# Seven products instead of eight in the gate and up projections of a two-layer decoder trunk

## The chip, the cores and the metric

The kernel runs on one core of one Trainium2 chip. The time is device time in microseconds for one execution, the median of repeated runs. Names of engines in the profile: PE is the matrix engine (TensorE) and PEld its weight loads, DVE is VectorE, ACT is ScalarE, POOL is GpSimd, SP is SyncE, on whose queue all transfers are issued.

## The reference

The program is a decoder trunk of 2 layers on 512 tokens of width 1024. Each layer is: x + 0.5·FFN1, a mixing part (a convolution group, a gated short convolution, a sparse attention group that keeps the 128 best keys), cross-attention into 256 memory tokens, x + 0.5·FFN2. A final RMS norm ends it. The part that the change touches is the FFN, four times in all (two per layer), with hidden width 2816:

```
def swiglu(h, w_gate, w_up, w_down):
    return (jax.nn.silu(h @ w_gate) * (h @ w_up)) @ w_down

x = x + 0.5 * swiglu(rms_norm(x, ffn1_norm[l]), ffn1_w_gate[l], ffn1_w_up[l], ffn1_w_down[l])
```

## The kernel before

Everything is kept transposed: features lie on the 128 partitions and the 512 tokens along the row. The 1024 features of x are 8 tiles X[0] to X[7], the 2816 hidden features are 22 columns of 128.

**Three matmuls for one product.** Every float32 factor is split into a high part that the matrix engine takes as it is (ACT copies it, rounded) and a low part (DVE subtracts the high part from the value). `mm3` then issues three matmuls: high·high, high·low, low·high. Each has its own weight load. A column of gate or up over 8 feature tiles is so 8·3 = 24 matmuls of 128x512.

**The norm.** `Norm.chunk` splits each x tile times its gain into `norm.h`; the factor 1/rms of each token (`norm.rb`) comes late, from `finish`: a sum of squares by POOL and PE, a power on POOL, and two matmuls with `ones_r` that spread it over the partitions. `norm.rb` is multiplied onto the gate and, after the down projection, onto the result.

**The FFN.** `ffn` works in two parts of 12 and 10 hidden columns (`HALVES`). In a part it first walks over column pairs: four weight blocks of 128x1024 (gate and up, two columns each) are loaded into `stg`, split into `whi` and `wlo`, and two columns of gate and two of up are computed. `gated` multiplies the gate by `norm.rb`, takes its silu, multiplies by up and splits the result into `hid`. Then the down projection of the part adds into X, in column pairs `mp`; the last part also calls `nxt.chunk`, which prepares the next norm. The first FFN of layer 0 begins with `begin`, which computes the first pair while x and the weights still arrive.

**What sets the order.** All operations are recorded first, as the functions call them. `Plan.order` then sorts them for all engines together: it gives each operation a cost and a due time (from the place of the matmuls that need it) and starts, engine by engine, the operation that is ready earliest, among equals that with the earliest due time. Buffers are counted: `stg` has 4, `whi` and `wlo` 3 each (NW), `s` 70 (NSLOT, 128x512 each), `ps` the 8 banks of PSUM. Each engine then executes its list strictly in this order, waiting on semaphores. Nearly all instructions show the same line (345 before, 353 after), the line that issues the sorted list; they are told apart by tiles and shapes.

Of the kernel before, what the change touches and what calls it, by code (L numbers as in the profile page):

```python
# [55 lines left out]
def _columns(c0, c1, k0=0, nk=DC, first=()):  # L56
    r, c = [], c0
    while c < c1:
        n = min(first[0] if first else P, c1 - c)
        first = first[1:]  # L60
        r.append((k0, nk, c, n))
        c += n
    return r


def _rows(c0, c1):
    return [(k, 2, c, T) for c in range(c0, c1, T) for k in range(0, DC, 2)]

BLOCKS = {"w_in": _columns(0, O_V) + _rows(O_V, O_QI) + _columns(O_QI, O_KI) + _columns(O_KI, N_IN, first=(68,)),
          "w_out": _columns(0, D), "xa_wq": _columns(0, D), "xa_wo": _columns(0, D),
          "xa_wkv": _columns(0, D) + _rows(D, 2 * D)}
for _name in ("ffn1", "ffn2"):
    BLOCKS[_name + "_w_gate"] = BLOCKS[_name + "_w_up"] = _columns(0, F, first=(2 * P,))
    BLOCKS[_name + "_w_down"] = [b for f0, nf in HALVES for i in range(2)
                                 for b in _columns(0, D, f0 + i * nf // 2, nf // 2)]

TWO_PI = 2.0 * math.pi  # L80
C1 = 6.28125
# [267 lines left out]
def trunk_kernel(ctx: ExitStack, tc: tile.TileContext, a: dict, out: bass.AP):  # L349
# [16 lines left out]
    def planned(pool, tag, w, dt):  # L366
        return nc.tile(tag, (P, w), dt, lambda: pool.tile([P, w], dt, tag=tag, name=nm(tag), bufs=nc.tags[tag]["bufs"]))
# [28 lines left out]

    def mm3(o, w, x, start, stop):
        nc.tensor.matmul(o, w[0], x[0], start=start, stop=False)
        nc.tensor.matmul(o, w[0], x[1], start=False, stop=False)
        nc.tensor.matmul(o, w[1], x[0], start=False, stop=stop)  # L400
# [36 lines left out]
    def pcol(name, i):  # L437
        return cols[:, COLS[name] + i:COLS[name] + i + 1]
# [65 lines left out]
    def block(w, k0, nk, c0, n):  # L504
        name, l = w
        at = 0
        for b0, bk, bc, bn in BLOCKS[name]:
            if b0 <= k0 and k0 + nk <= b0 + bk and bc <= c0 and c0 + n <= bc + bn:
                b = a[name][l][:, at:at + bk * bn].rearrange("p (k c) -> p k c", k=bk)
                return b[:, k0 - b0:k0 - b0 + nk, c0 - bc:c0 - bc + n]  # L510
            at += bk * bn

    def load(w, k0, nk, c0, n):

        stg = planned(wpool, "stg", 1024, F32)[:, :nk * n].fold(nk)
# [9 lines left out]
    def part(w, k, n=P):  # L525
        return w[0][:, k, :n], w[1][:, k, :n]


    def ffn(l, which, norm, nxt, begin=None, end=None):
        wg, wu, wd = ((f"{which}_w_{n}", l) for n in ("gate", "up", "down"))  # L530
        for f0, nf in HALVES:
            hid = []

            def gated(pg, pu):
                g = slot()
                nc.vector.tensor_mul(g, pg, norm.rb)
                s = slot()
                nc.scalar.activation(s, g, AF.Silu)
                nc.vector.tensor_mul(g, pu, s)
                hid.append(split(g))  # L540

            if begin and f0 == 0:
                begin(wg, wu)
                norm.finish()
                for ob in opening:
                    gated(*ob)
            for b in range(1 if begin and f0 == 0 else 0, nf // 2):
                c0 = (f0 + 2 * b) * P
                wgt = load_cols(wg, c0)
                wut = load_cols(wu, c0)  # L550
                for i in range(2):
                    pg, pu = bank(), bank()
                    for wt, o in ((wgt[i], pg), (wut[i], pu)):
                        for k in range(DC):
                            mm3(o, part(wt, k), norm.h[k], k == 0, k == DC - 1)
                    if f0 == 0 and b == 0 and i == 0:
                        norm.finish()
                    gated(pg, pu)
            for mp in range(DC // 2):
                kh = nf // 2  # L560
                ws = [load_cols(wd, mp * 256, 256, f0 + i * kh, kh) for i in range(2)]
                halves = end and f0 and mp == DC // 2 - 1
                for x in (slice(0, T // 2), slice(T // 2, T)) if halves else (slice(0, T),):
                    for i in range(2):
                        m = 2 * mp + i
                        o = bank()[:, x]
                        for k in range(nf):
                            mm3(o, part(ws[k // kh][i], k % kh), tuple(t[:, x] for t in hid[k]), k == 0, k == nf - 1)
# [567 lines left out]
```

## Time and profile before

| | us |
|---|---|
| median of 3 runs | 2278.47 (2278.05 to 2279.54) |
| the profiled execution | 2280.02 |
| its span, first to last instruction | 2278.2 |
| PE busy in the span | 2246.0 |
| DVE busy | 1273.3 |
| ACT busy | 844.8 |
| mean granted TensorE clock | 0.991 of full speed |

The program holds 10354 matmuls and as many weight loads. A busy time is the union of an engine's records. A matmul's record is longer than the step from one matmul to the next, since they are pipelined: the pace is read from start to start. DVE records also overlap a little with the next one.

### The profile page before, as it was taken

The page shows a single profiled execution, that of the slowest core. Times are in us where ns is not written, and L with a number is a line of the kernel's source. Part 1 is how long each engine was busy: PE and PEld are TensorE (multiplying, and loading weights), DVE is VectorE, ACT ScalarE, POOL GpSimd, SP SyncE. Part 2 cuts the span into 40 slices and gives each one's busy share as a digit, 9 for nine tenths or more (in the row PEclk, how much of TensorE's full clock was granted, in tenths as well). Part 3 has the DMA queues.
Part 4 walks back from the last instruction along what each step waited for, and adds up shares of the span by engine and source line. Part 5 has one row for each costly group of instructions (what it writes and reads, how often), then busy time and mean ns, then how long its engine had stood idle before and what let it go on. Part 6 is the DMA issues. An engine that isn't in the chain of part 4 may idle for free. (4 is left out here: it accounts for less than half of the span.)

```text
span 2278.2 us, 26623 instructions
## 1 busy us (share of the span) xinstructions
PE 2246.0 (99%) x10354; PEld 1854.7 (81%) x10354; DVE 1273.3 (56%) x2026; ACT 844.8 (37%) x1308; POOL 149.9 (7%) x111
## 2 busy tenths in 40 slices
PE   8999999998999999999999999999999999999998
PEld 7888888787688888888888888878787888888887
DVE  7334347999855544343543334469998554343434
ACT  5222334326834433222332223333377343222322
POOL 2000001101020200000100000020100101000001
PEclk9999999999999999999999999999999999999999
DMA  6333323445332232332333343243543313323322
GB/s 219 96 84 109 100 78 99 121 118 151 92 95 64 84 101 81 102 104 85 101 102 97 83 115 90 81 132 97 139 124 99 93 56 93 102 81 113 93 76 82
DMA packets 88335, 229.70 MB, mean 101 GB/s; under 512 B 10128, under 2 KB 23568, under 8 KB 88208
## 3 DMA queue, kind: packets, MB, share of 16 engines
q1 hardware_dynamic: 88208, 228.00, 34.8%
q8 instruction: 81, 1.33, 0.2%
q14 instruction: 46, 0.38, 0.1%
HBM read 211.70 MB, written 2.10 MB: 94 GB/s over the span
## 5 line engine op out<-in xcount | busy, mean ns | idle before, releaser
L345 PE MATMUL ps<-s,whi 128*128 128x512 f32 (+1 forms) x5896 | 1767.9, 385 | 0.0
L345 PEld LDWEIGHTS ps<-s,whi 128*128 128x128 f32 x5896 | 1098.2, 188 | 224.6 <-issue 4.4
L345 PE MATMUL ps<-s,wlo 128*128 128x512 f32 (+1 forms) x2948 | 1106.2, 384 | 0.0
L345 ACT ACTIVATE whi<-stg 128x1024 fp32r<-128x1024 f32 (+2 forms) x430 | 420.6, 979 | 1221.8 <-PE ps L345 1017.1
L345 PEld LDWEIGHTS ps<-s,wlo 128*128 128x128 f32 x2948 | 553.6, 188 | 108.9
L345 DVE TENSOR_TENSOR wlo<-stg,whi 128x1024 fp32r<-128x1024 f32 (+2 forms) x430 | 484.6, 1128 | 133.3 <-ACT whi L345 133.2
L345 DVE TENSOR_TENSOR s<-ps,s 128x512 f32<-128x512 f32 (+1 forms) x264 | 181.3, 690 | 566.1 <-PE ps L345 542.5
L345 POOL TENSOR_TENSOR s<-s,s 128x512 f32<-128x512 f32 (+1 forms) x88 | 134.7, 1534 | 1916.8 <-ACT s L345 1657.8
L345 ACT ACTIVATE s<-s 128x512 fp32r<-128x512 f32 (+2 forms) x255 | 157.0, 626 | 92.3 <-DMA s<-s 45.1
L345 PE MATMUL ps<-s,s 128*128 128x512 f32 (+7 forms) x688 | 162.0, 375 | 16.5 <-DVE s L345 12.1
L345 DVE TENSOR_TENSOR s<-s,s 128x512 fp32r<-128x512 f32 (+3 forms) x206 | 149.0, 732 | 7.7 <-ACT s L345 6.7
L345 DVE SCALAR_TENSOR_TENSOR s<-ps,s 128x512 f32<-128x512 f32 (+1 forms) x70 | 47.2, 676 | 187.4 <-PE ps L345 187.4
L345 PEld LDWEIGHTS ps<-s,s 128*128 128x128 f32 (+1 forms) x688 | 111.0, 187 | 46.4 <-DVE s L345 15.2
L345 ACT ACTIVATE s<-ps 128x512 fp32r<-128x512 f32 (+4 forms) x192 | 93.5, 534 | 70.1 <-PE ps L345 70.0
L345 DVE SCALAR_TENSOR_TENSOR s<-s,cols,s 128x256 fp32r<-128x256 f32 (+23 forms) x144 | 105.8, 767 | 0.4
L345 PE MATMUL ps<-whi,s 128*128 128x512 f32 x256 | 82.1, 395 | 0.0
L345 DVE SCALAR_TENSOR_TENSOR s<-x,cols,s 128x512 fp32r<-128x512 f32 x64 | 72.4, 1134 | 12.8 <-ACT s L345 11.2
L345 ACT ACTIVATE s<-s,sm 128x512 f32<-128x512 f32 (+3 forms) x128 | 65.0, 552 | 0.5 <-DVE sm L345 0.4
L345 PEld LDWEIGHTS ps<-whi,s 128*128 128x128 f32 x256 | 47.9, 188 | 12.8 <-issue 1.8
L345 DVE TENSOR_TENSOR x<-x,ps 128x512 f32<-128x512 f32 x32 | 22.0, 687 | 60.6 <-PE ps L345 60.6
L345 DVE MATCH_REPLACE8 s<-sm,s 128x256 f32<-128x256 f32 (+2 forms) x96 | 52.4, 561 | 0.0
L345 DVE MAX8 sm<-s 128x8 f32<-128x256 f32 (+2 forms) x96 | 51.3, 566 | 0.0
(69 smaller groups left out, 581.6 us busy)
## 6 DMA issues: line engine op xcount, KB each, us to landing
stg<-in_ffn_w_gate SPq DMA_DIRECT2D x86, 512.0 KB, 3.6
stg<-in_ffn_w_up SPq DMA_DIRECT2D x86, 512.0 KB, 3.6
stg<-in_ffn_w_down SPq DMA_DIRECT2D x64, 384.0 KB, 3.1
stg<-in_w_in SPq DMA_DIRECT2D x48, 512.0 KB, 3.6
stg<-in_ffn_w_down SPq DMA_DIRECT2D x64, 320.0 KB, 2.9
stg<-in_xa_wkv SPq DMA_DIRECT2D x32, 512.0 KB, 3.7
s<-s SPq DMA_DIRECT2D x64, 128.0 KB, 2.5
stg<-in_w_out SPq DMA_DIRECT2D x16, 512.0 KB, 3.6
```

The costliest lines, as they stand in the source:

```text
L345: getattr(getattr(nc, op.eng), op.name)(*map(real, op.args), **{k: real(v) for k, v in op.kw.items()})
```

## The change

For nine of the eleven column pairs of every FFN (all but the first two, `PLAIN = 2`) gate and up are computed by Strassen's scheme. One weight (gate or up) of a column pair is seen as a 2 by 2 block matrix: even or odd feature tiles by first or second column. The activations are a 2 by 2 block matrix too: even or odd feature tiles by first or second 256 tokens. Instead of eight block products of 4 feature tiles each there are seven, named A to G, each 4·3 = 12 matmuls of 128x256: 84 in place of 48 matmuls of 128x512 for a weight.

- `sevens` forms the sums of activations once for each FFN, now with `norm.rb` multiplied in, and splits them (the dictionary `x7`).
- `load_sevens` forms four sums of 128x512 for each weight on DVE and splits them: one tile for A and B, one for E and G, one for F and D, a half one for C. They need all 4 `whi` and `wlo` buffers (NW is now 4); the two sums have a pool `sum` of 2.
- `seven` runs the products in the order A, E, B, F, C, D, with G put off until after the next weight's A (`late`). The accumulations share three banks u, v, q: u takes A, then F, then D, then G on top of each other, and is read between them (`one`, `two`, `o`).
- `gated_sevens` replaces `gated` for these pairs; in `gated` itself one multiplication by `norm.rb` is added, so that the down projection needs none: X is updated by one DVE operation instead of two.
- The FFN has three parts of 8, 8 and 6 hidden columns (`PARTS`); each down block is a single load of 8 or 6 tiles instead of two of 6 or 5. NSLOT is 62.

```diff
-NSLOT = 70
+NSLOT = 62
 NSTG = 4
-NW = 3
+NSUM = 2
+NW = 4
-HALVES = ((0, 12), (12, 10))
+PARTS = ((0, 8), (8, 8), (16, 6))
+PLAIN = 2
...
+    def load_sevens(w, c0):
+        H = T
+        top, low, s23, s4 = (planned(wpool, g, 1024, F32) for g in ("stg", "stg", "sum", "sum"))
+        nc.sync.dma_start(top, half_quarters(w, c0, 0))
+        nc.sync.dma_start(low, half_quarters(w, c0, 1))
+        s4 = s4[:, :H]
+        nc.vector.tensor_sub(s23[:, H:], top[:, :H], low[:, :H])
+        nc.vector.tensor_add(low[:, :H], low[:, :H], low[:, H:])
+        nc.vector.tensor_sub(s23[:, :H], low[:, :H], top[:, :H])
+        nc.vector.tensor_sub(s4, top[:, H:], s23[:, :H])
+        r = {}
+        for t, names in ((top, "AB"), (low, "EG"), (s23, "FD"), (s4, "C")):
+            hl = split(t, *(planned(wpool, g, 1024, F32R)[:, :t.shape[-1]] for g in ("whi", "wlo")))
...
+    def sevens(norm):
+        H = T // 2
...
+        for j in range(DC // 2):
+            xe, xo = slot(), slot()
+            for i, x in enumerate((xe, xo)):
+                c = 2 * j + i
+                nc.vector.scalar_tensor_tensor(x, X[c], pcol(norm.gain, norm.i * DC + c), norm.rb, op0=ALU.mult,
+                                               op1=ALU.mult)
+            t12, t34 = slot(), slot()
+            nc.vector.tensor_sub(t12[:, :H], xe[:, H:], xe[:, :H])
+            nc.vector.tensor_sub(t12[:, H:], xo[:, H:], t12[:, :H])
+            nc.vector.tensor_sub(t34[:, :H], xo[:, H:], xe[:, H:])
+            nc.vector.tensor_sub(t34[:, H:], xo[:, :H], t12[:, H:])
...
+            r["A"].append(split(xe[:, :H], first[0][:, x], first[1][:, x]))
+            for t, names in ((xo, "BC"), (t12, "EF"), (t34, "DG")):
+                hl = split(t)
...
+        def seven(w, c0, x):
+            ws = load_sevens(w, c0)
+            u, v, q = (bank()[:, :H] for _ in range(3))
+            o = slot(), slot()
+            one, two = slot(), slot()
...
+            product(u, "A", True, True)
+            while late:
+                late.pop(0)()
+            nc.scalar.activation(one[:, :H], u, AF.Copy)
+            product(v, "E", True, True)
+            nc.scalar.activation(two[:, :H], v, AF.Copy)
+            product(q, "B", True, True)
+            nc.vector.tensor_add(o[0][:, :H], q, one[:, :H])
+            product(u, "F", False, True)
+            nc.scalar.activation(one[:, H:], u, AF.Copy)
+            product(v, "C", False, True)
+            nc.vector.tensor_add(o[0][:, H:], v, one[:, H:])
+            product(u, "D", False, True)
+            nc.vector.tensor_add(o[1][:, H:], u, two[:, :H])
+            late.append(lambda: product(u, "G", False, True))
+            return o, u
...
                 s = slot()
                 nc.scalar.activation(s, g, AF.Silu)
+                nc.vector.tensor_mul(s, s, norm.rb)
                 nc.vector.tensor_mul(g, pu, s)
...
+            def gated_sevens(g, u):
+                (ga, gb), gq = g
+                (ua, ub), uq = u
+                for x in (slice(0, H), slice(H, T)):
+                    nc.scalar.activation(ga[:, x], ga[:, x], AF.Silu)
+                nc.vector.tensor_mul(ua, ua, ga)
+                hid.append(split(ua))
+                nc.scalar.activation(gb[:, H:], gb[:, H:], AF.Silu)
+                nc.scalar.activation(gb[:, :H], gq, AF.Silu)
+                nc.vector.tensor_mul(ub[:, H:], ub[:, H:], gb[:, H:])
+                nc.vector.tensor_mul(ub[:, :H], uq, gb[:, :H])
+                hid.append(split(ub))
...
-                        t = slot()[:, x]
-                        nc.vector.scalar_tensor_tensor(t, o, 0.5, norm.rb[:, x], op0=ALU.mult, op1=ALU.mult)
-                        nc.vector.tensor_add(X[m][:, x], X[m][:, x], t)
-                        if f0:
+                        nc.vector.scalar_tensor_tensor(X[m][:, x], o, 0.5, X[m][:, x], op0=ALU.mult, op1=ALU.add)
+                        if last:
```

Three places show what this does to the sorted lists. The first is PE in the gate and up stage of the first FFN. Before, a column (`ps_140`) takes one feature tile after the other, three matmuls each:

```order
L345 MATMUL ps_140_651<-s_37_223,whi_135_623 128x512
L345 MATMUL ps_140_651<-s_41_235,whi_135_623 128x512
L345 MATMUL ps_140_651<-s_37_223,wlo_136_631 128x512
L345 MATMUL ps_140_651<-s_47_251,whi_135_623 128x512
L345 MATMUL ps_140_651<-s_51_264,whi_135_623 128x512
L345 MATMUL ps_140_651<-s_47_251,wlo_136_631 128x512
```

In the changed kernel, at the seam between two weights in the second part: `ps_521` is bank u of the next weight (the end of its A), `ps_527` its bank v (E), and `ps_508` bank u of the weight before (G).

```order
L353 MATMUL ps_521_2934<-s_130_560,whi_516_2891 128x256
L353 MATMUL ps_521_2934<-s_146_624,whi_516_2891 128x256
L353 MATMUL ps_521_2934<-s_130_560,wlo_518_2905 128x256
L353 MATMUL ps_527_2961<-s_136_583,whi_520_2925 128x256
L353 MATMUL ps_527_2961<-s_148_630,whi_520_2925 128x256
L353 MATMUL ps_527_2961<-s_136_583,wlo_522_2939 128x256
L353 MATMUL ps_508_2836<-s_174_750,whi_501_2776 128x256
L353 MATMUL ps_508_2836<-s_177_765,whi_501_2776 128x256
L353 MATMUL ps_508_2836<-s_174_750,wlo_502_2784 128x256
```

The matmuls have half the moving width, and G stands behind A and the first three matmuls of E.

The second place is DVE in the same stage. Before, a column pair holds its four low parts (`wlo`), a multiplication of the gate, one of up and a low part for each hidden column:

```order
L345 TENSOR_TENSOR s_142_663<-ps_134_615,s_104_451 128x512
L345 TENSOR_TENSOR wlo_143_668<-stg_121_536,whi_141_659 128x1024
L345 TENSOR_TENSOR s_142_663<-ps_140_651,s_144_671 128x512
L345 TENSOR_TENSOR wlo_148_702<-stg_127_572,whi_147_694 128x1024
L345 TENSOR_TENSOR s_150_711<-s_142_663,s_149_705 128x512
```

After, one weight's turn: `ps_552` is bank q (B), `ps_545` bank v (C), `ps_540` bank u (D) of the current weight; `wlo_559`, `wlo_564`, `wlo_568`, `wlo_574` are the low parts of the next one; `sum_571` and `stg_546` already belong to the one after that.

```order
L353 TENSOR_TENSOR s_557_3154<-ps_552_3120,s_548_3093 128x256
L353 TENSOR_TENSOR sum_558_3159<-stg_519_2919,sum_551_3116 128x512
L353 TENSOR_TENSOR wlo_559_3167<-stg_519_2919,whi_556_3148 128x1024
L353 TENSOR_TENSOR s_560_3180<-s_544_3082,s_555_3139 128x512
L353 TENSOR_TENSOR s_557_3154<-ps_545_3085,s_548_3093 128x256
L353 TENSOR_TENSOR wlo_564_3200<-stg_525_2956,whi_562_3186 128x1024
L353 TENSOR_TENSOR s_566_3214<-ps_540_3061,s_554_3131 128x256
L353 TENSOR_TENSOR wlo_568_3220<-sum_551_3116,whi_565_3205 128x1024
L353 TENSOR_TENSOR sum_571_3237<-stg_538_3045,stg_546_3087 128x512
L353 TENSOR_TENSOR stg_546_3087<-stg_546_3087 128x512
L353 TENSOR_TENSOR wlo_574_3255<-sum_558_3159,whi_572_3244 128x512
```

The reading of D (`ps_540`), for which G waits, now stands behind the low part of the next weight's E and G.

The third place is DVE at the start of FFN2 of layer 0, from the second spreading of 1/rms on (`ident`). Before, with `s_1305` as `norm.rb`:

```order
L345 TENSOR_SCALAR s_1302_6520<-ident_70,sm_1301_6517 128x128 x4
L345 TENSOR_TENSOR wlo_1304_6530<-stg_1275_6372,whi_1299_6506 128x1024
L345 TENSOR_TENSOR s_1307_6542<-ps_1283_6420,s_1305_6535 128x512
L345 TENSOR_TENSOR s_1307_6542<-ps_1290_6459,s_1308_6547 128x512
L345 TENSOR_TENSOR s_1311_6566<-ps_1297_6502,s_1305_6535 128x512
```

After, with `s_1482` as `norm.rb`:

```order
L353 TENSOR_SCALAR s_1479_7637<-ident_70,sm_1478_7634 128x128 x4
L353 TENSOR_TENSOR wlo_1481_7647<-stg_1452_7489,whi_1476_7623 128x1024
L353 TENSOR_TENSOR s_1484_7659<-ps_1460_7537,s_1482_7652 128x512
L353 SCALAR_TENSOR_TENSOR s_1485_7664<-x0_100,cols_98,s_1482_7652 128x512
L353 SCALAR_TENSOR_TENSOR s_1487_7671<-x2_102,cols_98,s_1482_7652 128x512
L353 SCALAR_TENSOR_TENSOR s_1489_7677<-x1_101,cols_98,s_1482_7652 128x512
L353 TENSOR_TENSOR s_1491_7684<-s_1485_7664 128x256
L353 TENSOR_TENSOR s_1486_7666<-s_1486_7666,s_1482_7652 128x512
```

The sums of `sevens` stand between the gatings of the first two column pairs.

## Rows read from the trace of the kernel before

**Rows 1.** The page's first part: busy us, share of the span, instructions
```profile
PE 2246.0 (99%) x10354; PEld 1854.7 (81%) x10354; DVE 1273.3 (56%) x2026; ACT 844.8 (37%) x1308; POOL 149.9 (7%) x111
```
**Rows 2.** Windows: stretch, length, busy us and instructions by engine, clock, DMA share, GB/s
```profile
456.00:513.00 57.00, 57.00 (x253) 47.22 (x252) 57.00 (x131) 16.84 (x22) 6.04 (x4) 1.00 0.45 121
684.00:741.00 57.00, 57.00 (x312) 49.30 (x310) 30.16 (x64) 25.33 (x56) 0.00 (x0) 1.00 0.21 63
2252.00:2261.60 9.60, 9.60 (x82) 9.60 (x81) 4.54 (x8) 2.25 (x4) 2.02 (x2) 1.00 0.00 0
798.00:1083.00 285.00, 285.00 (x1259) 236.08 (x1258) 112.57 (x134) 82.19 (x99) 0.00 (x0) 1.00 0.33 94
```
**Rows 3.** Timeline of PE, gate and up: start us, us, instruction, count
```profile
38.76 0.62 PE L345 MATMUL ps<-s,whi 128*128 128x512 f32 x2
39.21 0.39 PE L345 MATMUL ps<-s,wlo 128*128 128x512 f32 x1
...
41.48 0.62 PE L345 MATMUL ps<-s,whi 128*128 128x512 f32 x2
```
**Rows 4.** Timeline of PE, the half-width matmuls that end the last FFN
```profile
2256.71 0.40 PE L345 MATMUL ps<-s,whi 128*128 128x256 f32 x2
2256.95 0.28 PE L345 MATMUL ps<-s,wlo 128*128 128x256 f32 x1
...
2258.51 0.40 PE L345 MATMUL ps<-s,whi 128*128 128x256 f32 x2
```
**Rows 5.** Timeline of PEld in the same stretch
```profile
2256.59 0.31 PEld L345 LDWEIGHTS ps<-s,whi 128*128 128x128 f32 x2
```
**Rows 6.** Timeline of DVE, gate and up of FFN2, layer 0; idle before in brackets
```profile
1034.36 0.69 DVE L345 TENSOR_TENSOR s<-ps,s 128x512 f32<-128x512 f32 x1 [3.59 <-PE ps L345]
1034.98 1.23 DVE L345 TENSOR_TENSOR wlo<-stg,whi 128x1024 fp32r<-128x1024 f32 x1
1036.12 0.68 DVE L345 TENSOR_TENSOR s<-s,s 128x512 fp32r<-128x512 f32 x1
...
1045.24 0.69 DVE L345 TENSOR_TENSOR s<-ps,s 128x512 f32<-128x512 f32 x1 [3.64 <-PE ps L345]
```
**Rows 7.** Groups by form: count, busy us, mean ns, idle before and releasers
```profile
L345 DVE TENSOR_TENSOR wlo<-stg,whi 128x1024 fp32r<-128x1024 f32 x300 | 369.7, 1233 | 78.5 <-ACT whi L345 78.4
...
L345 DVE SCALAR_TENSOR_TENSOR s<-ps,s 128x256 f32<-128x256 f32 x4 | 1.6, 422 | 5.4 <-PE ps L345 5.4
...
L345 ACT ACTIVATE whi<-stg 128x1024 fp32r<-128x1024 f32 x300 | 317.6, 1061 | 857.8 <-PE ps L345 710.1 <-issue 141.7 <-DVE sm L345 4.4
...
L345 ACT ACTIVATE s<-ps 128x256 f32<-128x256 f32 x24 | 8.9, 408 | 0.0
...
L345 ACT ACTIVATE s<-s 128x512 fp32r<-128x512 f32 x142 | 88.6, 633 | 74.8 <-DMA s<-s 45.1 <-DVE s L345 19.6 <-DVE sm L345 2.3
```
**Rows 8.** Timeline of ACT and DVE, start of FFN2 in layer 0
```profile
782.61 0.69 DVE L345 TENSOR_TENSOR x<-x,ps 128x512 f32<-128x512 f32 x1 [2.86 <-PE ps L345]
...
787.64 1.06 ACT L345 ACTIVATE whi<-stg 128x1024 fp32r<-128x1024 f32 x1 [3.07 <-issue]
788.74 1.22 DVE L345 TENSOR_TENSOR wlo<-stg,whi 128x1024 fp32r<-128x1024 f32 x1 [3.55 <-ACT whi L345]
...
796.68 0.69 DVE L345 TENSOR_TENSOR s<-ps,s 128x512 f32<-128x512 f32 x1 [0.40 <-ACT s L345]
```
**Rows 9.** Timeline of DVE and PE, first FFN of layer 0
```profile
9.32 0.75 DVE L345 SCALAR_TENSOR_TENSOR s<-x,cols,s 128x512 fp32r<-128x512 f32 x1
9.98 1.87 DVE L345 TENSOR_TENSOR s<-s,s 128x256 fp32r<-128x256 f32 x2
...
33.62 0.50 PE L345 MATMUL ps<-s,ones_r 128*128 128x512 f32 x1 [3.31 <-DVE s L345]
...
37.21 1.29 DVE L345 TENSOR_TENSOR s<-ps,s 128x512 f32<-128x512 f32 x2 [0.40 <-ACT s L345]
37.84 0.40 PE L345 MATMUL ps<-s,whi 128*128 128x512 f32 x1
```

More of the change, by code (lines that the diff above doesn't have):

```diff
@@ L60, in _columns @@
         first = first[1:]
-        r.append((k0, nk, c, n))
+        r.append((k0, nk, c, n, 1))
         c += n
@@ L75 @@
 for _name in ("ffn1", "ffn2"):
-    BLOCKS[_name + "_w_gate"] = BLOCKS[_name + "_w_up"] = _columns(0, F, first=(2 * P,))
-    BLOCKS[_name + "_w_down"] = [b for f0, nf in HALVES for i in range(2)
-                                 for b in _columns(0, D, f0 + i * nf // 2, nf // 2)]
+    BLOCKS[_name + "_w_gate"] = BLOCKS[_name + "_w_up"] = (
+        _columns(0, PLAIN * 2 * P, first=(2 * P,)) + _quarters(PLAIN * 2 * P, F))
+    BLOCKS[_name + "_w_down"] = [b for f0, nf in PARTS for b in _columns(0, D, f0, nf)]
 TWO_PI = 2.0 * math.pi
@@ L356, in trunk_kernel @@
     nc = Plan(tc)
-    for tag, bufs, spare in (("s", NSLOT, 6), ("ps", 8, 2), ("sm", 24, 8), ("stg", NSTG, 9), ("whi", NW, 9),
-                             ("wlo", NW, 9)):
+    for tag, bufs, spare in (("s", NSLOT, 6), ("ps", 8, 2), ("sm", 24, 8), ("stg", NSTG, 9), ("sum", NSUM, 9),
+                             ("whi", NW, 9), ("wlo", NW, 9)):
         nc.pool(tag, bufs, spare)
@@ L395, in split, with mm3 @@
         return hi, lo
[L397 to L400, printed above, removed]
+    def mm3(o, w, x, start, stop, **kw):
+        nc.tensor.matmul(o, w[0], x[0], start=start, stop=False, **kw)
+        nc.tensor.matmul(o, w[0], x[1], start=False, stop=False, **kw)
+        nc.tensor.matmul(o, w[1], x[0], start=False, stop=stop, **kw)
     ident = const.tile([P, P], F32, name="ident")
@@ L506, in block @@
         at = 0
-        for b0, bk, bc, bn in BLOCKS[name]:
-            if b0 <= k0 and k0 + nk <= b0 + bk and bc <= c0 and c0 + n <= bc + bn:
+        for b0, bk, bc, bn, step in BLOCKS[name]:
+            if step == 1 and b0 <= k0 and k0 + nk <= b0 + bk and bc <= c0 and c0 + n <= bc + bn:
                 b = a[name][l][:, at:at + bk * bn].rearrange("p (k c) -> p k c", k=bk)
@@ L517, in load, with half_quarters @@
         return split(stg, *(planned(wpool, g, 1024, F32R)[:, :nk * n].fold(nk) for g in ("whi", "wlo")))
+    def half_quarters(w, c0, m):
+        name, l = w
+        at = 0
+        for b0, bk, bc, bn, step in BLOCKS[name]:
+            if step == 2 and b0 == 0 and bc == c0 + m * P:
+                return a[name][l][:, at:at + 2 * bk * bn]
+            at += bk * bn
+    def load_sevens(w, c0):
[11 more added lines that the diff above has]
+            hl = split(t, *(planned(wpool, g, 1024, F32R)[:, :t.shape[-1]] for g in ("whi", "wlo")))
+            for i, name in enumerate(names):
+                r[name] = [tuple(x[:, i * H + j * P:i * H + (j + 1) * P] for x in hl) for j in range(4)]
+        return r
     def load_cols(w, c0, n=256, k0=0, nk=DC):
@@ L529, in ffn, with product @@
     def ffn(l, which, norm, nxt, begin=None, end=None):
         wg, wu, wd = ((f"{which}_w_{n}", l) for n in ("gate", "up", "down"))
-        for f0, nf in HALVES:
+        H = T // 2
+        late = []
+        def seven(w, c0, x):
[3 more added lines that the diff above has]
+            one, two = slot(), slot()
+            def product(acc, name, start, stop):
+                for j in range(DC // 2):
+                    mm3(acc, ws[name][j], x[name][j], start and j == 0, stop and j == DC // 2 - 1,
+                        skip_group_check=True)
+            product(u, "A", True, True)
[14 more added lines that the diff above has]
+            return o, u
@@ L532, in ffn @@
+        for f0, nf in PARTS:
             hid = []
+            last = f0 + nf == FC
             def gated(pg, pu):
@@ L544, in ffn @@
                 norm.finish()
+                x7 = sevens(norm)
                 for ob in opening:
@@ L548, in ffn @@
                 c0 = (f0 + 2 * b) * P
[L549 to L558, printed above, removed]
+                if f0 == 0 and b < PLAIN:
+                    wgt = load_cols(wg, c0)
+                    wut = load_cols(wu, c0)
+                    for i in range(2):
+                        pg, pu = bank(), bank()
+                        for wt, o in ((wgt[i], pg), (wut[i], pu)):
+                            for k in range(DC):
+                                mm3(o, part(wt, k), norm.h[k], k == 0, k == DC - 1)
+                        if b == 0 and i == 0:
+                            norm.finish()
+                            x7 = sevens(norm)
+                        gated(pg, pu)
+                else:
+                    pair = [seven(w, c0, x7) for w in (wg, wu)]
+                    late.append(lambda pair=pair: gated_sevens(*pair))
+            while late:
+                late.pop(0)()
             for mp in range(DC // 2):
-                kh = nf // 2
-                ws = [load_cols(wd, mp * 256, 256, f0 + i * kh, kh) for i in range(2)]
-                halves = end and f0 and mp == DC // 2 - 1
+                ws = load_cols(wd, mp * 256, 256, f0, nf)
+                halves = end and last and mp == DC // 2 - 1
                 for x in (slice(0, T // 2), slice(T // 2, T)) if halves else (slice(0, T),):
```

18 lines of the change are left out of this document (14 added, 4 removed).

## Prediction

> **What bounds the kernel now.** I read the page's first part, then windows, then timelines of single stages. PE is busy for 2246.0 of the 2278.2 us [rows 1], so the question in every stage is only whether PE waits. In the down, gate and up stages it never does: from 798 to 1083 us PE is busy all 285.0 us at full clock, DVE 112.57 and ACT 82.19 us [rows 2]. The other window to look at is 456 to 513, in the mixing: there DVE too is busy for all 57.00 us, and PE still for all 57.00 [rows 2]. So a nearly full DVE doesn't by itself hold PE up. The timeline gives the pace: from 38.76 to 41.48 four groups of three 512-wide matmuls start, 2.72 us / 12 = 226.7 ns each [rows 3]. What the change needs is the pace at 256 columns, and the trace has it: from 2256.71 to 2258.51 five groups of three, 1.80 us / 15 = 120.0 ns each [rows 4], with the same high, high, low pattern and one weight load per matmul. The loads keep up there: PEld starts one every 120 ns, each with a record of 190 ns that overlaps the next [rows 5]. The clock stays full in that stretch and in 684 to 741, where half-width matmuls are many [rows 2].
>
> **PE's work.** The tail's halves shift a little as well (72 instead of 120 half-width matmuls there, 24 more full ones). In all 3432 matmuls of 512 columns go and 6000 of 256 come: -3432 x 226.7 + 6000 x 120.0 = -777.9 + 720.0 = **-57.9 us**. Over a third of the 92 us that an eighth fewer columns would give (3456 x 213.3 / 8) is eaten, since each matmul costs 13.3 ns beyond its columns at 2.4 GHz (226.7 - 213.3, and 120.0 - 106.7), and there are more of them. For one weight of a pair: 84 x 120 = 10.08 us in place of 48 x 226.7 = 10.88.
>
> The Trainium skill bears on this ("TensorE: Matmul & The Clock Gate", Back-to-back issue gap): it gives columns / 2.4 GHz plus 2.5 ns, so 215.8 and 109.2 ns; by it the sum would be -3432 x 215.8 + 6000 x 109.2 = -85.4 us, an estimate. The trace has 226.7 and 120.0 for the same two widths, so the measurement decides. The same page of the Trainium skill (LDWEIGHTS, loading the stationary operand) puts a weight load at its columns over 1.2 GHz, 106.7 ns for 128, which speaks against narrow matmuls; the trace's loads every 120 ns leave it just hidden.
>
> **DVE beside it, for one weight.** Durations overlap when DVE has its next work: 0.62 us from start to start at 512 columns and 1.14 at 1024 [rows 6]; at 256 the record is 0.42 [rows 7], so some 0.34, an estimate by the same overlap. Four sums 4 x 0.62; low parts 3 x 1.14 + 0.62; three readings of banks 3 x 0.34; half of a pair's gating (0.62 + 2 x 0.34 + 2 x 0.62) / 2 = 1.27. Together 2.48 + 4.04 + 1.02 + 1.27 = **8.8 us of 10.08**, where before a weight had two low parts and three other 512-wide operations, 2 x 1.14 + 3 x 0.62 = 4.1 of 10.88. ACT for one weight: 3 x 1.06 + 0.63 of high parts, three bank copies and two silus of 0.41, one high part of 0.63 [rows 7]: 6.5 of 10.08. Both fit, DVE with 1.3 us to spare. The loads are the same blocks of 512 KB at 33% DMA share [rows 2], on the same four `stg` buffers; the down loads get fewer (24 for 32 in an FFN).
>
> **The wait that the change adds.** With four `whi` buffers a weight tile is split when a product frees its buffer. Three products lie between the freeing and the use of A/B, E/G and C (4.3 us), four for F/D; ACT and DVE need 1.10 from high to low part [rows 8] and 1.14. The tight one is G: it may only accumulate after DVE has read D, and that reading is queued behind the low part of the next E/G, whose buffer C frees. From C's end: 1.10 + 1.14 + 0.42 = 2.66 us, plus two semaphore hops. PE meanwhile has D, the next A and three matmuls of E: 1.44 + 1.44 + 0.36 = 3.24. So 0.58 us for two hops, which no row shows by itself. Behind a late G stands the rest of E on PE, and behind it everything. I take 0.03 us for each of the 72 weights, **+2 us**; ends 0 and 0.3 each, 22 us (nothing can be gained: PE's work is fixed).
>
> **The starts of the FFNs.** `sevens` is 8 operations of 0.67 (9.32 to 9.98 [rows 9]), 16 of 0.34, and low parts of 12 x 0.62 + 4 x 0.34: 19.6 us of DVE after `norm.rb`. In FFN2 of layer 0 the projection before ends near 782.5, the first multiplication by `norm.rb` comes at 796.68 [rows 8]; two plain pairs last 4 x 10.88 = 43.5, to 826. In the new DVE list 32 operations stand from there to the last that A needs: 9 x 0.62 + 8 x 0.67 + 3 x 1.14 + 12 x 0.34 = 18.4 us, so 815. All of x7 takes 28 more: 18 x 0.62 + 2 x 1.14 + 8 x 0.34 = 16.2, so 831.3; its last part is for D and G, and D begins 5 products on, at 833.2. It fits with 2 us to spare. I take 0.7 us for each of three such starts. Layer 0's first FFN has only one plain pair: `norm.rb` is used at 37.21, PE starts the pair at 37.84 [rows 9], so A could start at 59.6. The same walk ends x7 at 70.2, D should start at 66.8; PE has part of D and the next A to fill in: 1 us of waiting there and 2 more in the next weight. Against it, ten more matmuls now stand ahead of the first `ones_r` matmul on PE, which waited 3.31 us [rows 9]: -2.3. Together +1. **All four starts +3 us**, from -2 to 34 (8 each).
>
> **The edges of the parts.** One more part per FFN means one more time from pairs to down and back. The last gating takes some 2.5 us after G (0.41 + 0.34 + 0.63 + 0.62 and hops); the down's first column has six finished hidden columns to work on, 18 x 0.2267 = 4.1 us. I take 0.5 for each of the four, **+2 us** (0 to 10). The plain gatings' extra multiplication (4 x 0.62 per FFN) and the shorter update of X are DVE work under PE and cost nothing; if that cover goes they are part of the rival below. Mixing: the list of layer 1 is nearly unchanged, in layer 0 memory-key matmuls move among the attention's; PE idles 32 us in the whole span [rows 1], so a change of 4 us either way; value 0.
>
> **Sum.** 2280.0 (profiled execution) - 57.9 + 2 + 3 + 2 = 2229.1. That execution lies 1.5 above the median of the runs, so **2227.6 us**, own range 2217 to 2240.
>
> **Rivals.**
> *DVE becomes the bound in the nine pairs, and the kernel gets slower.* Place: the DVE list of one weight; point: when it takes over 10.88 us, PE loses more than it won. With records end to end instead of overlapped: 4 x 0.69 + 3 x 1.23 + 0.70 + 3 x 0.42 + 1.45 = 9.9, and if each of the four low parts stands 0.3 us waiting for ACT's high part, 11.1 us; then 72 x (11.1 - 10.08) = 73 more: 2280.0 - 57.9 + 73 - 1.5 = 2294. For it: 87% full, in order, and freed buffers come just in time. Against it: the window of full DVE with full PE [rows 2], and a turn that I could lay out without a gap on PE. 0.12 (over the line 0.09, equal 0.02, a small gain 0.01).
> *Starts and edges wait.* 8 us at each of the four starts and 0.3 us for half of the weights: 2222.1 + 32 + 11 - 1.5 = 2264 at worst, 2240 to 2264. For it: x7 is 19.6 us of new DVE work with 2 us to spare. Against: it needs only its A part at first. 0.13.
> *Half-width matmuls closer than 120 ns*, or the mixing wins: were the 13.3 ns halved, 6000 x 6.7 = 40 us less, 2187. Against it: 82 such matmuls start in 9.60 us [rows 2]. 0.03. (The pace that the Trainium skill's page "TensorE: Matmul & The Clock Gate" gives lies on this side.)
>
> **Chances.** Forecast 0.72, the others 0.12, 0.13, 0.03. The measurement can't tell less than about 0.2%, 4.6 us, from no change. Faster: 0.72 + 0.13 + 0.03 + 0.01 = 0.89; same 0.02; slower 0.09. The range 2212 to 2254 leaves out the third rival, most of the first, and the worst of the second: not quite 0.2.
>
> **What would show it.** Right: starts of 256-wide matmuls 120 ns apart over nine pairs, a weight every 10.1 us, PE without waits there, DVE near 87%, clock 1.0. The G wait would show as PE waiting on DVE once per weight, just after three matmuls of E; the start as PE waiting on DVE in D of the first weight. Wrong: a weight taking 10.5 us or more with DVE at 100%, a pace other than 120 ns, or new idle time of PE in the mixing.

## The result, and the profile after

The changed kernel takes 2217.04 us (2214.69 to 2217.16), the kernel before in the same comparison 2278.70 (2278.05 to 2279.54): the ratio is 0.9727, 95% interval 0.971 to 0.9744. The forecast was 2227.6, with 2217 to 2240 as its own range, so the gain of 62 us came out some 11 us larger than forecast, just at the edge.

The page's first part, after; it answers to [rows 1]:

```profile
PE 2183.5 (99%) x12922; PEld 1928.6 (87%) x12922; DVE 1675.1 (76%) x2748; ACT 1063.5 (48%) x1772; POOL 153.1 (7%) x111
```

PE is still busy for 99% of the span (now 2215.3 us), and lost 62.5 us of work by its records. DVE rose from 56% to 76%.

Windows of after (stretch, length, busy us and instructions of PE, PEld, DVE, ACT, POOL, then clock, DMA share, GB/s), to be set beside [rows 2]: all of FFN2 of layer 0, two stretches of nine-pair stages, and the beginning of the nine pairs in layer 0's first FFN:

```profile
773.10:1120.00 346.90, 346.90 (x2243) 318.34 (x2242) 252.44 (x374) 165.75 (x254) 11.35 (x8) 1.00 0.35 101
912.00:969.00 57.00, 57.00 (x476) 57.00 (x475) 49.21 (x74) 33.97 (x57) 0.00 (x0) 1.00 0.38 110
1995.00:2052.00 57.00, 57.00 (x476) 57.00 (x475) 51.08 (x78) 33.76 (x57) 0.00 (x0) 1.00 0.36 103
57.00:114.00 57.00, 55.65 (x397) 52.58 (x396) 53.76 (x92) 32.18 (x54) 1.09 (x1) 0.97 0.38 112
```

In a nine-pair stage 475 matmuls of 256 columns pass in 57.00 us (the row's 476 counts one that lies across its edge), 120.0 ns each, the pace of [rows 4]. PE has no idle time there, or in the whole FFN of the first row, though DVE is busy for 86 to 90%. Only the last row has gaps (1.35 us) and a clock under 1.00.

DVE in one nine-pair stage of after (start, us, instruction, idle before); compare [rows 6]:

```profile
929.25 1.22 DVE L353 TENSOR_TENSOR wlo<-stg,whi 128x1024 fp32r<-128x1024 f32 x1 [0.48 <-ACT whi L353]
931.30 0.42 DVE L353 TENSOR_TENSOR s<-ps,s 128x256 f32<-128x256 f32 x1 [0.84 <-PE ps L353]
931.76 0.69 DVE L353 TENSOR_TENSOR s<-s,s 128x512 f32<-128x512 f32 x1
...
949.47 1.23 DVE L353 TENSOR_TENSOR wlo<-stg,whi 128x1024 fp32r<-128x1024 f32 x1 [0.48 <-ACT whi L353]
```

The first and the last row are the same operation two weights apart: 20.22 us, so 10.11 for a weight. DVE finds time to wait for PE and ACT. The groups by form of after have the new small operations at or below the durations of [rows 7] (ACT's copies of a bank take 378 ns where 408 was used):

```profile
L353 DVE TENSOR_TENSOR s<-ps,s 128x256 f32<-128x256 f32 x252 | 104.9, 420 | 88.2 <-PE ps L353 88.2
L353 DVE TENSOR_TENSOR wlo<-sum,whi 128x1024 fp32r<-128x1024 f32 x72 | 87.7, 1219 | 0.0
L353 ACT ACTIVATE s<-ps 128x256 f32<-128x256 f32 x276 | 103.4, 378 | 93.3 <-PE ps L353 92.8
```

What PE waited for in the whole span of after (us, times, longest):

```profile
PE ps L353 <- DVE s L353: 18.7, 11, 6.4
PE ps L353 <- ACT s L353: 2.4, 4, 0.8
PE ps L353 <- DVE sm L353: 1.7, 2, 1.0
PE ps L353 <- DVE ones L414: 1.1, 1, 1.1
PE ps L353 <- DVE wlo L353: 0.5, 1, 0.5
```

Nothing recurs 72 times, so no wait for G shows; the 658 matmuls of a stage of eight weights, in a window shown further below, pass in 79.09 us, 120.2 ns each. The span, cut at PE's first `ones` matmul of each FFN norm and at the mixing's first 68-column matmul (us; two runs of the next section beside it):

| stretch | before | after | all pairs plain | before, four buffers |
|---|---|---|---|---|
| FFN1, layer 0 | 376.1 | 365.8 | 373.5 | 373.6 |
| mixing, layer 0 | 414.2 | 407.3 | 409.2 | 409.7 |
| FFN2, layer 0 | 360.5 | 346.9 | 360.5 | 360.5 |
| FFN1, layer 1 | 350.8 | 337.1 | 350.7 | 350.7 |
| mixing, layer 1 | 411.3 | 407.7 | 408.4 | 407.8 |
| FFN2, layer 1 | 351.4 | 337.7 | 351.3 | 351.3 |
| tail | 13.9 | 12.8 | 12.8 | 13.2 |

The four FFNs won 51.2 us. The other 11.7 us came from the mixings and the tail, for which the forecast had zero.

### The profile page after: what moved, and what is told of

Same layout as the page of the kernel before. It is cut to its first block, busy times and chain, and to the rows that moved or that the text cites. A ratio compares the mean times of both kernels' runs of the same rounds, so it can differ in the third digit from the quotient of the medians.

```text
span 2215.3 us, 32854 instructions
## 1 busy us (share of the span) xinstructions
PE 2183.5 (99%) x12922; PEld 1928.6 (87%) x12922; DVE 1675.1 (76%) x2748; ACT 1063.5 (48%) x1772; POOL 153.1 (7%) x111
## 5 line engine op out<-in xcount | busy, mean ns | idle before, releaser
L353 PE MATMUL ps<-s,whi 128*128 128x256 f32 (+2 forms) x7608 | 1770.4, 330 | 0.8 <-DVE s L353 0.8
L353 PEld LDWEIGHTS ps<-s,whi 128*128 128x128 f32 (+1 forms) x7608 | 1265.0, 190 | 137.1 <-issue 4.3
L353 PE MATMUL ps<-s,wlo 128*128 128x256 f32 (+2 forms) x3804 | 1176.0, 330 | 0.5 <-DVE wlo L353 0.5
L353 PEld LDWEIGHTS ps<-s,wlo 128*128 128x128 f32 (+1 forms) x3804 | 693.6, 190 | 64.7 <-DVE wlo L353 0.7
L353 ACT ACTIVATE whi<-stg 128x1024 fp32r<-128x1024 f32 (+1 forms) x398 | 413.1, 1042 | 694.1 <-PE ps L353 481.0
L353 DVE TENSOR_TENSOR wlo<-stg,whi 128x1024 fp32r<-128x1024 f32 (+1 forms) x398 | 476.0, 1197 | 102.7 <-ACT whi L353 102.3
L353 DVE TENSOR_TENSOR s<-ps,s 128x256 f32<-128x256 f32 (+2 forms) x372 | 186.0, 506 | 108.6 <-PE ps L353 88.2
L353 ACT ACTIVATE s<-ps 128x256 f32<-128x256 f32 (+4 forms) x444 | 188.0, 444 | 154.5 <-PE ps L353 153.6
L353 DVE TENSOR_TENSOR s<-s,s 128x512 fp32r<-128x512 f32 (+4 forms) x406 | 252.9, 647 | 6.3 <-ACT s L353 4.1
L353 ACT ACTIVATE s<-s 128x512 fp32r<-128x512 f32 (+3 forms) x355 | 188.8, 546 | 112.6 <-DVE s L353 77.5
L353 PE MATMUL ps<-s,s 128*128 128x512 f32 (+7 forms) x688 | 151.8, 365 | 15.9 <-DVE s L353 14.4
L353 DVE SCALAR_TENSOR_TENSOR s<-x,cols,s 128x512 fp32r<-128x512 f32 (+1 forms) x96 | 96.7, 1019 | 13.2 <-ACT s L353 11.5
L353 DVE TENSOR_TENSOR x<-x,ps 128x512 f32<-128x512 f32 x32 | 22.0, 686 | 57.6 <-PE ps L353 57.6
```

Of the source, the lines that this page charges most:

```text
L353: getattr(getattr(nc, op.eng), op.name)(*map(real, op.args), **{k: real(v) for k, v in op.kw.items()})
```

## The experiments

Two questions: what bounds the nine pairs, and where the 11 us come from.

**The change without its seven products.**

```diff
-PLAIN = 2
+PLAIN = 11
...
-                x7 = sevens(norm)
...
-                if f0 == 0 and b < PLAIN:
+                if c0 < PLAIN * 2 * P:
...
-                        if b == 0 and i == 0:
+                        if f0 == 0 and b == 0 and i == 0:
                             norm.finish()
-                            x7 = sevens(norm)
```

> All eleven column pairs by the plain 512-wide matmuls; everything else of the change stays (three parts, norm.rb in the gating, one-operation update of X, 62 slots, four whi and wlo buffers). Theory: the seven products gave 57.6 us of PE work and cost about 4 us at the first FFN's start; the other 8 to 11 us of the gain lie in the two mixing parts and the tail and come with the rest of the change, so this run is at 2217 + 57.6 - 4 = 2271 (2267 to 2273), 7 to 11 us below the kernel before. Rival: the mixing gained only because of what the sevens do to the order ahead of it; then this run is at 2278, like the kernel before.

2268.80 us, ratio 0.9954 (0.9939 to 0.9969). The theory held: everything but the seven products wins 10.9 us against the kernel before in the same comparison (2279.67), and the table shows that none of it is in the three FFNs behind the first. The seven products by themselves are so worth 51.8 us (2268.80 to 2217.04), where the whole forecast was a gain of 50.9.

**One product more on PE.** The product B is issued twice into its bank.

```diff
-            product(q, "B", True, True)
+            product(q, "B", True, False)
+            product(q, "B", False, True)
```

> Product B is issued twice onto its bank (the result of B is doubled), so eight products of 12 matmuls per weight; nothing else changes. Theory (PE alone bounds the nine pairs, 120 ns a matmul, DVE beside it): 72 x 12 x 0.120 = 103.7 us more, 2321. Rival (DVE or the waits on buffers share the bound, so that more PE work is partly hidden): clearly less, under 2300.

2320.22 us, ratio 1.0177 (1.0156 to 1.0197), 103 us above the changed kernel where 72 x 12 x 0.120 = 103.7. So PE's work goes into the time in full, at 120 ns a matmul. The three later FFNs show it one by one: they grew by 25.8, 25.9 and 26.1 us, where 18 x 12 x 0.120 = 25.9 was added to each.

**More work on DVE**: two, four or eight extra operations per weight, the first kernel with the two lines shown here, the last with each of four such lines twice.

```diff
         nc.vector.tensor_sub(s23[:, H:], top[:, :H], low[:, :H])
+        nc.vector.tensor_tensor(s23[:, H:], s23[:, H:], s23[:, H:], op=ALU.max)
...
         nc.vector.tensor_sub(s4, top[:, H:], s23[:, :H])
+        nc.vector.tensor_tensor(s4, s4, s4, op=ALU.max)
```

> Two more 512-wide DVE operations for each weight of the nine pairs (the maximum of a sum with itself, which leaves the value as it is). Theory: DVE goes from 8.8 to 10.0 us of 10.08 per weight, PE still bounds but the gaps are gone: 2217 to 2235. Rival (DVE is the bound already, or the just-in-time buffers let nothing more in): 72 x 1.24 = 89 us more, 2306.

2217.74 us, ratio 0.973 (0.9714 to 0.9746): no cost.

> Four more such DVE operations for each weight. Theory: 8.8 + 4 x 0.62 = 11.3 us per weight, over PE's 10.08, so DVE bounds the nine pairs: 72 x (11.3 - 10.08) = 87 us more, 2304 (2285 to 2320), at the price of the kernel before or above it. If DVE has more hidden room than I counted: under 2270.

2228.03 us, ratio 0.9772 (0.9753 to 0.9792): 11 us above the changed kernel where 87 were expected, a miss. Windows of this run, in the second part of FFN2 of layer 0, and over the whole first nine-pair stage of that FFN:

```profile
912.00:969.00 57.00, 57.00 (x476) 57.00 (x476) 56.97 (x90) 32.55 (x51) 0.00 (x0) 1.00 0.28 93
812.18:853.12 40.94, 39.48 (x322) 38.82 (x321) 40.94 (x67) 23.73 (x41) 0.00 (x0) 1.00 0.26 78
```

DVE is full in the first window, some 11.3 us of work for each weight, and PE passes 476 matmuls all the same. The extra work is late, but it is not yet late for PE: sums of the next part are made while PE does the down projection, and gatings of the last pairs are done in it. Of the three stages of an FFN only the first, beside the forming of x7, became longer (40.94 for 38.59). From this came a rule with numbers, tested by the third kernel:

> Every weight of a nine-pair stage gets eight extra 512-wide maxima of a tile with itself on DVE (0.60 us from start to start each in the run with four of them), so DVE needs about 8.9 + 4.8 = 13.7 us per weight, PE still 10.08. Theory A (the limit is set over a part, and the sums of two weights can be made ahead while PE does the down projection): a part with 8 weights owes 8 x 3.6 = 29 us less 2 x 7.3 made ahead = 14; with 6 weights 7; the first part of an FFN, 4 weights and the x7 sums beside them, 0 to 8. Per FFN about 26, four FFNs 104: 2217 + 104 = 2321 us (2285 to 2360). Theory B (my rival's rule: each weight waits for its own DVE list): 72 x 3.6 = 261, so 2478 (2450 to 2500). Theory C (only DVE's total counts: 1675 + 576 x 0.60 = 2021 us, still under PE's 2184): below 2240.

2370.76 us, ratio 1.0404 (1.0385 to 1.0423), 154 above the changed kernel. The three nine-pair stages of FFN2 of layer 0, with 4, 8 and 6 weights, in the changed kernel:

```profile
809.43:848.02 38.59, 38.59 (x323) 38.59 (x322) 34.32 (x53) 23.89 (x41) 0.00 (x0) 1.00 0.29 83
893.39:972.48 79.09, 79.09 (x658) 79.08 (x657) 63.43 (x93) 46.26 (x77) 0.00 (x0) 1.00 0.33 94
1017.86:1076.95 59.09, 59.09 (x490) 58.92 (x489) 45.05 (x66) 32.75 (x57) 0.00 (x0) 1.00 0.29 81
```

and with the eight operations:

```profile
846.58:900.14 53.56, 45.16 (x322) 42.74 (x321) 51.57 (x86) 24.49 (x44) 0.00 (x0) 0.90 0.20 60
945.52:1040.23 94.71, 86.33 (x658) 83.95 (x657) 92.35 (x145) 45.11 (x77) 0.00 (x0) 0.95 0.27 79
1085.60:1152.46 66.86, 61.92 (x491) 60.53 (x489) 65.63 (x104) 33.52 (x57) 0.00 (x0) 0.97 0.24 72
```

The stages grew by 15.0, 15.6 and 7.8 us. DVE is busy for 96 to 98% of each of these windows, so it is DVE that sets their length; PE's waits and its clock of 0.90 to 0.97 are the same lost time seen from PE. That DVE works ahead shows in its groups by form in the down projection between the first two windows (900.14 to 945.52), where eight of the extra maxima of sums, six to a weight, are done for weights of the next part:

```profile
L353 DVE TENSOR_TENSOR sum<-sum 128x512 f32<-128x512 f32 x8 | 5.5, 687 | 0.1
```

The rule gave 14 for the second and 7 for the third, which fits; for the first it gave 0 to 8, too little: there DVE has x7 to form, and nothing was made ahead. The sum, 38 per FFN in place of 26, missed its range by 11 us; the rule that each weight waits for its own list (2478) and the rule of DVE's total (under 2240) missed by far more.

**One plain pair less in every FFN.**

```diff
-PLAIN = 2
+PLAIN = 1
```

> Ten instead of nine pairs by seven products (PLAIN = 1), so the first FFN has no plain pair after its opening and the other three have one. PE's work falls by 4 x 2 x (48 x 226.7 - 84 x 120.0 ns) = 6.4 us. Theory (the two plain pairs are what hides the forming of x7): A of the first weight waits for its part of x7 and D for the rest, by the walk of the prediction 15 to 20 us at each of three starts and about 26 at the first FFN: 2217 - 6 + 45 to 60 + 26 = 2280 to 2297, value 2288. Rival (the sorted list puts the low parts and gatings behind x7, and the starts wait little): at most 5 us each, 2210 to 2231. PE should show waits on DVE s right behind the first plain pair under the theory.

2252.38 us, ratio 0.9885 (0.9866 to 0.9903), between the theory and its rival. The first nine-pair stage of FFN2 of layer 0 (6 weights now), as a window:

```profile
799.88:867.05 67.17, 63.13 (x490) 60.82 (x489) 61.70 (x102) 39.60 (x68) 0.00 (x0) 0.97 0.26 79
```

PE's timeline has the longest wait there, for operands of x7:

```profile
802.21 0.39 PE L353 MATMUL ps<-s,whi 128*128 128x256 f32 x1 [1.33 <-DVE s L353]
```

The same six weights take 59.09 in the third stage above, so this start costs 8 us, not 15 to 20. The plain pairs do hide x7. Why the rest is hidden with one pair less isn't shown; I take it that DVE's list puts off more other work than I had walked through.

**One plain pair more in the first FFN alone**, from the tiles that were loaded for the seven products.

```diff
+    def load_quarters(w, c0):
...
-                if f0 == 0 and b < PLAIN:
-                    wgt = load_cols(wg, c0)
-                    wut = load_cols(wu, c0)
+                extra = begin and f0 == 0 and b == PLAIN
+                if f0 == 0 and (b < PLAIN or extra):
+                    wgt = load_quarters(wg, c0) if extra else load_cols(wg, c0)
+                    wut = load_quarters(wu, c0) if extra else load_cols(wu, c0)
...
```

> Only the first FFN of layer 0 gets a second plain pair after its opening (the two columns of its first nine-pair weight computed with 512-wide matmuls from the same loaded tiles), everything else stays. Theory (its start waits 4.9 us of PE time, half-clock stretch included, because only one plain pair hides x7): the wait goes, 1.6 us of PE work come back: -3 us against the changed kernel, 2214 (2211.5 to 2216). Rival (the wait only moves to the next thing that is late, or the clock's half stretch comes elsewhere): 2217 to 2220.

2216.42 us, ratio 0.9729 (0.9716 to 0.9742): the same as the changed kernel. The start did become clean:

```profile
57.00:114.00 57.00, 57.00 (x332) 50.57 (x331) 46.15 (x72) 28.10 (x42) 0.00 (x0) 1.00 0.33 99
```

The first FFN ends 4.5 us earlier (361.3), but the mixing behind it takes 410.2 us in place of 407.3, with 13.7 us at the half clock (a granted clock of 1.2 in place of 2.4 GHz) where the changed kernel has 10.2, and 12.8 us of waits of PE for 10.7. The rival held: most of the gain was given back elsewhere.

**What the mixing gained from**: each of three remaining parts of the change put alone into the kernel before. First the shorter update of X:

```diff
+                nc.vector.tensor_mul(s, s, norm.rb)
...
-                        t = slot()[:, x]
-                        nc.vector.scalar_tensor_tensor(t, o, 0.5, norm.rb[:, x], op0=ALU.mult, op1=ALU.mult)
-                        nc.vector.tensor_add(X[m][:, x], X[m][:, x], t)
+                        nc.vector.scalar_tensor_tensor(X[m][:, x], o, 0.5, X[m][:, x], op0=ALU.mult, op1=ALU.add)
```

> The kernel before with one part of the change alone: the silu is multiplied by norm.rb in the gating, and X is updated by one DVE operation in place of two. Theory (this shortens the way from the last matmul of a down projection to the next norm by one DVE operation of 0.6 us at each FFN's end, and the tail's 1 us): 2278.5 - 4 = 2274.5 (2272 to 2277). Rival (it is the cause of the whole 11 us won in the mixing and the tail, because PE then idles less before the clock falls): 2266 to 2270. Rival (nothing): 2278 to 2279.5.

2277.73 us, ratio 0.999 (0.9981 to 1.0): 1.9 us less than the kernel before in the same comparison (2279.63), at most some 4 us, and hardly to be told from nothing.

Then the pools:

```diff
-NSLOT = 70
+NSLOT = 62
-NW = 3
+NW = 4
```

> The kernel before with the pool sizes of the change alone: four whi and four wlo buffers in place of three (NW), 62 slots in place of 70. Theory (the fourth buffer lets the mixing's weights be split earlier, so that PE has less idle time there and fewer stretches at the half clock): -6 us, 2272.5 (2269 to 2275). Rival (pools make no difference in the mixing): 2277 to 2280; with eight slots less it could also be slower, 2280 to 2285.

2268.73 us, ratio 0.9952 (0.9937 to 0.9966): 10.9 us, as much as the change without its seven products won, and nearly twice what the theory gave. By the table 8.0 us of it lie in the two mixings, 0.7 in the tail and 2.5 in the first FFN of layer 0. The number of buffers and the number of slots were changed together, so which of the two did it isn't shown.

Then the parts of the FFN:

```diff
-HALVES = ((0, 12), (12, 10))
+PARTS = ((0, 8), (8, 8), (16, 6))
...
-                kh = nf // 2
-                ws = [load_cols(wd, mp * 256, 256, f0 + i * kh, kh) for i in range(2)]
...
+                ws = load_cols(wd, mp * 256, 256, f0, nf)
...
```

> The kernel before with one part of the change alone: three parts of 8, 8 and 6 hidden columns and whole down blocks, all pairs with 512-wide matmuls, three whi and wlo buffers, 70 slots, the update of X by two operations. Theory (neither gains nor costs in the FFNs, as one more edge costs PE nothing; the order in the mixing is nearly the same): 2278.5 (2275.5 to 2281). Rival (the shorter last part frees slots and the next norm earlier, and is what the mixing gained from): 2268 to 2273.

2283.71 us, ratio 1.0019 (1.001 to 1.0029): 4 us slower, somewhat more than expected, and its mixings are 3.5 and 3.1 us longer than before. Their time at the half clock is that of the kernel before, 30.7 us; PE's waits in them are 23.8 us in place of 18.0.

Part of how the pools win time shows in the mixing of layer 0. PE in the kernel before, where the attention's small matmuls begin:

```profile
609.93 0.39 PE L345 MATMUL ps<-whi,s 128*128 128x512 f32 x1
610.16 1.84 PE L345 MATMUL ps<-ones,s 128*128 128x1 f32 x16
612.23 2.88 PE L345 MATMUL ps<-ident,s 128*128 128x128 f32 x13 [0.23 <-ACT s L345]
615.98 0.76 PE L345 MATMUL ps<-s,ones_r 128*128 128x512 f32 x1 [0.88 <-DVE sm L345]
...
618.60 3.06 PE L345 MATMUL ps<-s,s 128*64 128x512 f32 x6
```

and with the pools of the change:

```profile
605.58 0.28 PE L345 MATMUL ps<-ones,s 128*128 128x1 f32 x2
605.72 0.71 PE L345 MATMUL ps<-whi,s 128*128 128x512 f32 x2
606.26 0.73 PE L345 MATMUL ps<-ones,s 128*128 128x1 f32 x6
606.85 0.47 PE L345 MATMUL ps<-wlo,s 128*128 128x512 f32 x1
...
613.48 1.07 PE L345 MATMUL ps<-s,s 128*64 128x512 f32 x4
```

Windows of before around that place:

```profile
612.80:614.50 1.70, 1.56 (x11) 0.92 (x11) 1.40 (x4) 1.70 (x5) 0.92 (x1) 1.00 0.01 5
614.50:621.30 6.80, 5.92 (x18) 2.90 (x17) 4.46 (x14) 5.26 (x14) 0.00 (x0) 0.50 0.28 80
```

and of the kernel with the pools, where the same attention matmuls pass:

```profile
610.50:617.30 6.80, 6.63 (x29) 2.74 (x29) 5.25 (x15) 6.13 (x15) 0.00 (x0) 1.00 0.16 61
```

Before, the 512-wide matmuls are used up when the 16 one-column and the transposing `ident` matmuls come; after some 4 us of these alone the granted clock falls to the lower level (1.2 GHz) for 6.8 us, and a 512-wide attention matmul there takes twice the time (six in 2.99 us to the next start, 0.50 each; with the pools four in 1.00 us, 0.25 each). With the pools of the change, wide matmuls of a split weight stand between the small ones, and the clock stays at 2.4 GHz: 29 matmuls pass in 6.80 us in place of 18. Over both mixings the time at the half clock is 30.7 us before, 17.1 with the pools, and 17.1 in the changed kernel. That it isn't the luck of one trace shows in the mean granted clock of every execution: 0.990 to 0.994 in 19 of the kernel before, 0.994 to 0.996 in four with the pools. In a stretch at the half clock of the changed kernel (70.70 to 74.11, shown in the next section) 16 matmuls of 256 columns pass in 3.41 us, 213 ns each for 120, so 44% of that time is lost; by this, 13.6 us less are worth an estimated 6.0. The Trainium skill ("TensorE: Matmul & The Clock Gate", HAM oscillation — how this bites in real kernels) counts half of the throttled time as lost; by it they are worth an estimated 6.8. The two mixings of the table won 8.0, and PE's waits in them grew a little, from 18.0 to 19.2 us, so 2 to 3 us are explained by neither. That the wide matmuls in between are what kept the clock up is read from these two traces; no run put them there alone.

**A fifth buffer**, as a try for a faster version: in the changed kernel, and in the one with the extra plain pair.

```diff
-NSLOT = 62
+NSLOT = 58
-NW = 4
+NW = 5
```

> The changed kernel with five instead of four whi and wlo buffers (NW = 5) and 58 instead of 62 slots. In the nine-pair stages PE has no waits left, so nothing can come there. Theory (it was the buffer count that won the 11 us of the mixing, because split weights then lie ready beside the small matmuls of its attention; the changed kernel still has 10.2 and 6.8 us at the half clock there, and 4.9 us of waits at its first start): one of the stretches of 6.8 us goes, 3.4 us: 2213.5 (2209 to 2216). Rival (four were enough, the stretches left come from waits that no weight can fill): 2216 to 2219. Rival (four slots less hold up something): 2219 to 2225.

> As the run with five whi and wlo buffers and 58 slots, and with the second plain pair in the first FFN of layer 0. The run with that pair and four buffers left its first FFN 4.5 us earlier and lost 2.9 us of it in the mixing of layer 0 (13.7 us at the half clock there in place of 10.2). Theory (the fifth buffer fills that): 4.5 us under the changed kernel, 2212.5 (2209 to 2215). Rival (the two do not add): 2215 to 2219.

2260.77 us, ratio 0.992 (0.9905 to 0.9935), and 2248.45, ratio 0.9866 (0.9849 to 0.9882): 44 and 31 us slower than the changed kernel, against every expectation. PE's timeline in the first of them, in the mixing of layer 0:

```profile
571.84 0.80 PE L353 MATMUL ps<-s,s 128*128 128x256 f32 x2 [33.24 <-DVE sm L353]
```

and DVE's in the time that PE waits:

```profile
540.99 7.15 DVE L353 SCALAR_TENSOR_TENSOR s<-s,cols,s 128x502 f32<-128x502 f32 x11
...
552.77 9.86 DVE L353 SCALAR_TENSOR_TENSOR s<-s,cols,s 128x494 f32<-128x494 f32 x13
...
571.09 0.68 DVE L353 CUSTOM_DVE_ANT_0 s<-ps,s 128x512 f32<-128x512 f32 x1
```

The sorted list now has the convolution's chain on DVE ahead of the attention's reading of its scores, and at its end two operations that wait 3.41 us for a transfer and 1.16 us for POOL; PE stands for 33.24 us behind it; its FFNs are as long as in the changed kernel (FFN2 of layer 0: 346.8). Whether the fifth buffer or the four slots less turned the order stays open: both were changed at once. None of the twelve runs is measurably faster than the changed kernel.

## Why the prediction was right, and where it was not

- **PE's work, -57.9.** Right. The swap is 14.4 us for an FFN; the three later ones became 13.6, 13.7 and 13.7 us shorter. The pace of 120.0 ns came out as read from [rows 4], and the run with B twice priced it by itself. The rival with a closer pace fell: no stretch here reached 109.2 ns. That figure is from the formula columns / 2.4 GHz plus 2.5 ns of the Trainium skill's page "TensorE: Matmul & The Clock Gate" (Back-to-back issue gap); the section calls it the gap of a single matmul, which leaves out the weight loads, so it wasn't a forecast for a stream with one load per matmul, as the prediction took it.
- **The wait for G, +2.** It came to nothing that shows: no wait recurs with the weights, and their pace is 120.2 ns a matmul.
- **Starts +3 and edges +2.** Together with G 7; measured 51.2 for 57.6, so 6.4. That the sums nearly agree is luck. The three later FFNs lost only 0.8, 0.7 and 0.7, where I had some 1.7 each, and the first lost 4.2 of its 14.4, where start, G and edge together were 2. It would be 6.7 against the run with all pairs plain, which already has the pools' 2.5 us in that FFN. PE waits twice for the late end of x7, as the walk had it (PE's timeline of after, idle before in brackets):

```profile
68.20 0.39 PE L353 MATMUL ps<-s,whi 128*128 128x256 f32 x1 [0.84 <-DVE s L353]
69.94 0.39 PE L353 MATMUL ps<-s,wlo 128*128 128x256 f32 x1 [0.51 <-DVE wlo L353]
```

  Behind that the granted clock is at half for 3.4 us, which I hadn't counted (and once before, at 36.6, as it is in the kernel before at 34.2); the window of that stretch:

```profile
70.70:74.11 3.41, 3.41 (x16) 3.01 (x16) 3.41 (x7) 2.75 (x5) 0.00 (x0) 0.51 0.00 0
```

  This clock isn't a fixed cost of the start: the trace of the run with B twice has no stretch at the half clock in this FFN, and the FFN grew by 22.3 us there, 3.6 less than was added to it.

  And the earlier wait at `ones_r` shrank from 3.31 us [rows 9] to 2.45 only, not by 2.3; PE's timeline after:

```profile
35.27 0.50 PE L353 MATMUL ps<-s,ones_r 128*128 128x512 f32 x1 [2.45 <-DVE s L353]
```

- **Mixing, value 0, "a change of 4 us either way".** This term was mis-sized: it measured -11.7 with the tail. I had looked at instructions and idle time of PE, and both hardly changed. What changed is the time at the half clock, which explains most of it, and the cause is in the main the pool sizes, which I had read as a need of the seven products only: the run with the pools alone won 8.7 us in the same stretches. The last 3 us, nearly all in the mixing of layer 0, no run singles out.
- **The rival of a full DVE.** Its place was right and its point wrong. "When it takes over 10.88 us, PE loses more than it won" takes each weight by itself. With 11.3 us per weight PE lost 11 us in all. What counts is a part: its overhang, less some 14 us, which the balance leaves for work made ahead under the down projection (29 - 15.6, and 21.6 - 7.8), and without that help in the first part of an FFN.

## What to carry to other kernels

Price a swap of many narrow for fewer wide instructions by the start-to-start pace of each width in the trace. An engine beside the bound one may be overloaded for a while: reckon its debt from one stage to the next, less what it can do ahead. And where a change touches pool sizes in a kernel whose order is sorted by a program, run the pool sizes alone: here they were a sixth of the gain, and one step further they cost more than half of it.

## What the runs showed of the hardware

PE's clock fell to the half level right behind a stretch in which PE was busy by its records for 1.56 of 1.70 us, but with 1- and 128-column matmuls; so the granted clock has to be read beside the busy time. And DVE ran 56.97 of 57.00 us beside a PE that was busy for all of it at 120 ns a matmul, so the two didn't slow each other there.
